# Raw weight buffers, load distance and the engine of the weight sums in the down stage of an MLP

## The chip, the cores and the metric

The kernel runs on one core of one Trainium2 chip. The metric is the device time of one execution in microseconds (us); it is the median of several runs. One further execution was recorded by the hardware profiler, and all rows come from that one.

## The reference, cut to what matters

Two layers work on 1024 + 32 = 1056 tokens of 1024 features: layer a has a state-space mixer, layer b a stick-breaking attention. Each layer ends with the same MLP, and this is all that the change touches:

```python
def sq_relu_mlp(h, w_up, w_down):
    return jnp.square(jax.nn.relu(h @ w_up)) @ w_down

for i in range(DEPTH):                       # DEPTH = 2
    ...                                      # mixer i, y += mixer(rmsnorm(y))
    y_p = y_p + sq_relu_mlp(rms_norm(y_p, norm_mlp[i]), mlp_up[i], mlp_down[i])
    y_s = y_s + sq_relu_mlp(rms_norm(y_s, norm_mlp[i]), mlp_up[i], mlp_down[i])
```

`w_up` is 1024 x 4096 and `w_down` 4096 x 1024, both float32.

## The kernel before

Activations lie transposed: features on the 128 partitions, the 1056 tokens along the free dimension, so a tile of 128 features is [128, T] with T = 1056; HW = 528 is half of the tokens, QW = 264 a quarter. `X[d]` for d = 0 to 7 is the residual stream, kept in SBUF.

Matrix products are made exact enough by splitting each float32 operand into a rounded part (`hi`, made by ScalarE) and a remainder (`lo`, made by VectorE), and by adding three products hi*hi, hi*lo, lo*hi on TensorE. One product of the MLP (`product`, L849) runs for each of its k operands three such pairs over two token quarters, so 6 matmuls of 128 x 264 per operand; with four operands these are 24 matmuls.

In the MLP a two-by-two block product is done with seven products instead of eight. This needs sums of the quarters of the weights. `wprep` (L798 to L844) makes the weights of one step in seven parts: `load` brings two raw tiles of 128 x 1024 from DRAM (`ws_...`, in buffers of the rotation `ws`, which holds two of them); `sums1` has a subtraction on GpSimd (L818, it writes half of the tile `wS`) and an addition in place on VectorE (L819); `sums2` has a subtraction on VectorE (L823) and one on GpSimd (L825, into a tile of its own, `wS4`); then four `split` parts, raw0, S, raw1 and S4, each with a rounding on ScalarE (L835) and a remainder on VectorE (L836). Where a step has fewer than four operands the tiles are narrower: 128 columns per operand and quarter.

The up stage (`project`, L971) goes through 15 pairs of output tiles; a pair has seven products of four operands. During pair p the weights of pair p+1 are made, one part after each product. The results, squared, go to DRAM as `q_d[k]` (seven halves of 528 tokens for each k = 0 to 15).

The down stage goes through 19 steps (`STEPS`). Step s adds the products of the operands in `ks` to one pair of output tiles d1, d2 of `X`. Steps 0 to 18 have 2, 3, 4, 4, 3, 3, 3, then nine times 4 (steps 7 to 15), then 3, 2 and 1 operands. In `step` (L1003) the seven products use three PSUM tiles: U, W, U, V, U, V, U. After each product VectorE adds the tile to half of an `X` tile (L1018). So the third product can't begin to write U before the addition of the first is done, the fifth not before that of the third, and the sixth not before that of the fourth. Beside product n run the n-th part of a refill and the n-th part of the weights of the next step. A refill (`refill`, L983) reads the seven halves `q_d[k]` (L993) into four tiles `y` and splits them (L718 on ScalarE, L719 on VectorE) into the operand buffers of a k that is used up. Refills r0, r1 and r2 are the operands 0, 1 and 2; r0 and r1 are made during the last pair of the up stage, r2 beside step 0, operand 3 beside step 1, and 4 to 15 beside steps 3 to 14 (step 2 and steps 15 to 18 have none). `reload` (L1063) brings the eight X tiles back from DRAM (L1066).

All DMAs are issued on SP's queue, in order. Each engine, too, takes its instructions in order. In the MLP that order isn't written out by hand: a scheduler lays the instructions out when the program is built, by their place in the source and by its own reckoning of when operands and buffers are free, so an instruction can stand in its queue well ahead of its place in the source. Waits follow from the data and from buffers being reused.

Of the kernel before, what the change touches and what calls it, by code (L numbers as in the profile page):

```python
# [7 lines left out]
F32 = mybir.dt.float32  # L8
# [4 lines left out]
ALU = mybir.AluOpType  # L13
# [5 lines left out]
T = SEQ + DEC  # L19
# [4 lines left out]
HW = T // 2  # L24
# [68 lines left out]
def hybrid_step(ctx: ExitStack, tc: tile.TileContext, xt, cst, cbf, w_in, w_dt, w_out, w_up0, w_dn0, w_qkv, w_o,  # L93
# [27 lines left out]
    rota = {"ws": [0, 1], "wh": [0, 1, 2], "wl": [0, 1, 2]}  # L121

    def wtile(kind, dt, name):

        n = rota[kind].pop(0)
        rota[kind].append(n)
        return wp.tile([128, 1024], dt, name=f"{kind}_{name}", tag=f"{kind}{n}")

    eng = [ve]
# [495 lines left out]
    def mlp_pools(st, stp, name):  # L625
        mp = st.enter_context(tc.tile_pool(name=f"mp{name}", bufs=2, reuse_waits="tile"))
        pp = stp.enter_context(tc.tile_pool(name=f"pp{name}", bufs=8, space=PSUM, reuse_waits="tile"))
        return mp, pp
# [35 lines left out]
    class Up:  # L664
# [132 lines left out]

        def wprep(self, p, loads, n=4):  # L798


            w = {}
            nm = f"{self.name}{p}"

            def view(t):
# [7 lines left out]
            def part(t, i):  # L812
                return t[:, 512 * i:512 * i + 128 * n]

            def sums1():
                r0, r1 = w["raw0"], w["raw1"]
                S = w["S"] = self.mp.tile([128, 1024], F32, name=f"wS_{nm}", tag="wS", bufs=1)
                gp.tensor_tensor(part(S, 1), part(r0, 0), part(r1, 0), op=ALU.subtract)  # L818
                ve.tensor_tensor(part(r1, 0), part(r1, 0), part(r1, 1), op=ALU.add)  # L819

            def sums2():
                r0, r1, S = w["raw0"], w["raw1"], w["S"]
                ve.tensor_tensor(part(S, 0), part(r1, 0), part(r0, 0), op=ALU.subtract)  # L823
                S4 = w["S4"] = self.mp.tile([128, 512], F32, name=f"wS4_{nm}", tag="wS4", bufs=1)
                gp.tensor_tensor(part(S4, 0), part(r0, 1), part(S, 0), op=ALU.subtract)  # L825

# [12 lines left out]
            def ready():  # L839
                (a, b, s, q) = (w[f"{x}_"] for x in ("raw0", "raw1", "S", "S4"))  # L840
                self.prepared[p] = [(a, 0), (s, 0), (a, 512), (s, 512), (b, 0), (b, 512), (q, 0)]

            return [load, sums1, sums2, lambda: split("raw0"), lambda: split("S"), lambda: split("raw1"),
                    lambda: (split("S4"), ready())]  # L844

# [124 lines left out]

        def project(self, tail):  # L971

            for p in range(1, 16):
                prep = self.up_weights(p + 1) if p < 15 else tail
                if p == 1:
                    prep.insert(3, self.mix0)
                self.pair(p, prep)

# [3 lines left out]

        def refill(self, k):  # L983

            box = {}

            def f(j):
                n = ORDER.index(j)
                if n % 2 == 0:
                    box["y"] = self.mp.tile([128, T], F32, name=f"y_{self.name}{k}{j}", bufs=2 if n < 4 else 1,  # L990
                                            tag=("sq", "sq", "acc", "u0")[n // 2])
                    for i, jj in enumerate(ORDER[n:n + 2]):
                        dma(box["y"][:, HW * i:HW * i + HW], self.q_d[k, QPOS.index(jj)])  # L993
                t = self.ttile(DTAGS[k % 4][n], f"d{j}_{self.name}{k}")
                self.split(j, ("d", k), box["y"][:, HW * (n % 2):HW * (n % 2) + HW], t[:, 0:HW], t[:, HW:T])

            return [lambda j=j: f(j) for j in ORDER]

        def down_weights(self, s):
            pair, ks = STEPS[s]  # L1000
            return self.wprep(f"d{s}", lambda i: self.w_dn[pair, i][:, :, 128 * ks[0]:128 * ks[-1] + 128], len(ks))

# [22 lines left out]
    def mlp(X, src, w_last, gain_col, w_up, w_dn, mp, pp, close_pp, stp, name, order, last=None, each=None):  # L1025

        up = Up(mp, name, gain_col, w_up, order)
        xs = [up.parts(src[i], (f"m{2 * i}", f"m{2 * i + 1}"), f"l{name}{i}") for i in range(4)]
        blk = down_block(w_last, xs, X, pp, f"l{name}", lambda d: up.add(d, X[d]))
# [29 lines left out]
        hold = [f"h{order[d]}" for d in (0, 1, 3, 5, 2, 4, 6, 7)]  # L1059
        r0, r1, r2 = (up.refill(k) for k in range(3))  # L1060
        dw = up.down_weights(0)

# [5 lines left out]
        with ExitStack() as pu:  # L1068
            up.psum = pu.enter_context(tc.tile_pool(name=f"pu{name}", bufs=4, space=PSUM, reuse_waits="tile"))
            up.project([lambda: (dw[0](), reload((0, 1))), dw[1], lambda: (run(r0[:3]), dw[2]()),  # L1070
                        lambda: (run(r0[3:6]), dw[3]()), lambda: (run(r0[6:] + r1[:3]), dw[4]()),
                        lambda: (run(r1[3:5]), dw[5](), reload((2, 3))), lambda: (dw[6](), run(r1[5:]))])
        reload(range(4, KD))
# [4 lines left out]
        with ExitStack() as pd:  # L1078
            up.psum = pd.enter_context(tc.tile_pool(name=f"pd{name}", bufs=1, space=PSUM, reuse_waits="tile"))
            up.roles = {"U": 0, "V": 2, "W": 3, "F": 1}  # L1080
            for s, (pair, _) in enumerate(STEPS):
# [593 lines left out]
```

## Time and profile before

| | us |
|---|---|
| median of 3 runs | 3089.58 (3088.73 to 3091.41) |
| profiled execution | 3097.83 |
| its span, first to last instruction | 3096.1 |
| down stage of layer a | 1310.6 to 1692.4 |
| down stage of layer b | 2727.5 to 3092.2 |

The profile names engines PE (TensorE matmuls), PEld (its weight loads), DVE (VectorE), ACT (ScalarE), POOL (GpSimd) and SP (the DMA queue). A row of the timeline has the start in us, the duration in us, the engine, the line of the kernel, the operation, the tile written, the tiles read, their sizes and how many instructions are merged in the row; in brackets, how long the engine had been idle before, and what it waited for. Times within the profile count from the first instruction. Tiles of layer a carry an a in their name, those of layer b a b; `ws_ad`, `wh_ad`, `wl_ad`, `wS_ad` are the down stage's raw weights, rounded weights, remainders and sums, `d_a` its operands, `ps_da9U` the PSUM tile U of step 9, `x_sa` the saved X.

### The profile page before, as it was taken

The numbers are of one execution on the slowest core, as the hardware profiler recorded it, in microseconds if no ns is written. First come the engines' busy times: TensorE is split into PE (matmuls) and PEld (weight loads), VectorE is DVE, ScalarE is ACT, GpSimd is POOL, SyncE is SP. The second block draws the span as 40 slices with busy tenths as digits, with TensorE's granted clock in tenths as the row PEclk, the third lists the DMA queues.
The fourth block names the chain that finished last, engine by engine and source line by source line (L and its number), as shares of the span: only waits on it lengthen the run. The fifth ranks groups of instructions, "written<-read, shape, count | busy, mean of one in ns | idle before, by whom it ended". The sixth has DMA issues, their size and how long they took to land.

```text
span 3096.1 us, 55134 instructions
## 1 busy us (share of the span) xinstructions
PE 2962.8 (96%) x22206; PEld 2809.7 (91%) x22206; DVE 2272.8 (73%) x3192; ACT 1292.1 (42%) x2207; POOL 851.6 (28%) x667
## 2 busy tenths in 40 slices
PE   9999999999999999989998999999999999989999
PEld 7899888898999999989998888888889999989999
DVE  7877778776749877767677677677678877777675
ACT  4433333434214333334333466666664433344331
POOL 2666656665100111011112023333230111111111
PEclk9999999999999999989999999999999999999999
DMA  4323333333522544554432322222234444474442
GB/s 133 71 74 77 72 79 82 81 79 93 184 90 103 176 153 143 172 182 151 136 113 93 105 78 75 66 71 71 78 119 141 150 143 139 143 240 145 128 139 84
DMA packets 191351, 360.11 MB, mean 116 GB/s; under 512 B 21772, under 2 KB 78968, under 8 KB 191096
## 3 DMA queue, kind: packets, MB, share of 16 engines
q1 hardware_dynamic: 191096, 356.59, 37.5%
q8 instruction: 175, 2.87, 0.4%
q14 instruction: 80, 0.66, 0.1%
HBM read 246.21 MB, written 101.93 MB: 112 GB/s over the span
## 4 chain that ended last, share of the span: by engine, by line
PE 64%; DVE 20%; DMA 5%; issue 5%; ACT 3%; POOL 2%; SPq 0%; DVEq 0%; POOLq 0%; ACTq 0%
PE ps_i L181 9%; PE ps_ub L857 9%; PE ps_ua L857 8%; PE ps_q L181 3%; PE ps_o L181 3%; PE ps_k L181 2%; PE o L1356 2%; PE wt L1340 2%; PE ps_v L181 2%; PE ps_o L162 2%; PE ps_lb L162 1%; PE ps_p L181 1%; DVE p L1303 1%; DMA ws_ad<-in_w_dn 1%; PE ps_la L162 1%
## 5 line engine op out<-in xcount | busy, mean ns | idle before, releaser
L181 PE MATMUL ps_i<-xh_n,wh_i 128*128 128x352 f32 x1056 | 359.9, 341 | 0.0
L181 PE MATMUL ps_i<-xl_n,wh_i 128*128 128x352 f32 x1056 | 344.4, 326 | 0.0
L181 PE MATMUL ps_i<-xh_n,wl_i 128*128 128x352 f32 x1056 | 344.3, 326 | 0.0
L1305 POOL TENSOR_TENSOR b<-b,p 128x255 f32<-128x255 f32 (+7 forms) x128 | 165.3, 1292 | 377.7 <-DVE p L1303 243.1
L1303 DVE TENSOR_TENSOR_SCAN p<-p 128x255 f32<-128x255 f32 (+7 forms) x128 | 193.2, 1510 | 90.6 <-ACT p L1301 89.5
L181 PEld LDWEIGHTS ps_i<-xh_n,wh_i 128*128 128x128 f32 x1056 | 202.4, 192 | 13.3 <-issue 11.6
L181 PEld LDWEIGHTS ps_i<-xl_n,wh_i 128*128 128x128 f32 x1056 | 203.5, 193 | 0.0
L181 PEld LDWEIGHTS ps_i<-xh_n,wl_i 128*128 128x128 f32 x1056 | 202.0, 191 | 0.0
L466 ACT ACTIVATE L<-L,naT 128x128 f32<-128x128 f32 (+1 forms) x288 | 89.7, 382 | 166.5 <-POOL L L463 166.5
L818 POOL TENSOR_TENSOR wS_a<-ws_a,ws_a 128x512 f32<-128x512 f32 x15 | 24.9, 1661 | 387.0 <-DMA ws_a<-in_w_up 372.8
L1301 ACT ACTIVATE p<-z,qn_q 128x384 f32<-128x384 f32 (+4 forms) x192 | 104.6, 579 | 60.0 <-PE z L1332 30.1
L140 POOL TENSOR_TENSOR wl_i<-ws_i,wh_i 128x1024 fp32r<-128x1024 f32 x44 | 105.4, 2395 | 73.7 <-ACT wh_i L139 73.5
L463 POOL TENSOR_TENSOR L<-ab,cs 128x512 f32<-128x512 f32 (+1 forms) x72 | 103.1, 1433 | 52.9 <-PE pb L498 43.4
L718 ACT ACTIVATE d_b<-y_b 128x528 fp32r<-128x528 f32 x112 | 70.8, 640 | 110.6 <-DMA y_b<-q_db 16.5
L718 ACT ACTIVATE d_a<-y_a 128x528 fp32r<-128x528 f32 x112 | 70.7, 640 | 107.1 <-DMA y_a<-q_da 13.8
L1340 PE MATMUL wt<-cs,b 128*128 128x128 f32 x576 | 90.4, 281 | 14.8 <-DVE wts L1345 12.3
L1301 ACT ACTIVATE b<-z,qn_q 128x384 f32<-128x384 f32 (+4 forms) x192 | 104.3, 584 | 0.0
L818 POOL TENSOR_TENSOR wS_bd<-ws_bd,ws_bd 128x512 f32<-128x512 f32 (+3 forms) x19 | 21.9, 1153 | 296.4 <-DMA ws_bd<-in_w_dn 272.1
L818 POOL TENSOR_TENSOR wS_b<-ws_b,ws_b 128x512 f32<-128x512 f32 x15 | 24.0, 1600 | 284.6 <-DMA ws_b<-in_w_up 254.6
L818 POOL TENSOR_TENSOR wS_ad<-ws_ad,ws_ad 128x512 f32<-128x512 f32 (+3 forms) x19 | 23.3, 1225 | 275.6 <-DMA ws_ad<-in_w_dn 255.8
L719 DVE TENSOR_TENSOR d_b<-y_b,d_b 128x528 fp32r<-128x528 f32 x112 | 82.0, 742 | 21.6 <-ACT d_b L718 20.9
L719 DVE TENSOR_TENSOR d_a<-y_a,d_a 128x528 fp32r<-128x528 f32 x112 | 81.0, 735 | 18.4 <-ACT d_a L718 17.5
(1650 smaller groups left out, 9734.9 us busy)
## 6 DMA issues: line engine op xcount, KB each, us to landing
y_a<-q_da SPq DMA_DIRECT2D x112, 264.0 KB
y_b<-q_db SPq DMA_DIRECT2D x112, 264.0 KB
ws_i<-in_w_in SPq DMA_DIRECT2D x48, 512.0 KB
ab<-acs_d SPq DMA_DIRECT2D x64, 256.0 KB
q_da<-t_a SPq DMA_DIRECT2D x30, 528.0 KB
q_db<-t_b SPq DMA_DIRECT2D x30, 528.0 KB
ws_a<-in_w_up SPq DMA_DIRECT2D x30, 512.0 KB
ws_b<-in_w_up SPq DMA_DIRECT2D x30, 512.0 KB
```

What stands on the lines that cost most here:

```text
L140: eng[0].tensor_tensor(lo, st, hi.bitcast(F32), op=ALU.subtract)
L162: te.matmul(box["ps"][g][:, :GW], a[:, c:c + 128], b[:, GRP[g]], start=(k == ks[0] and i == 0), stop=(k == ks[-1] and i == 2))
L181: te.matmul(box["ps"][:, :n], a[:, c:c + 128], b[:, grp[g]], start=(k == 0 and i == 0), stop=(k == nk - 1 and i == 2))
L463: gp.tensor_tensor(L[0:w, :, :w], ab[0:w, :, :w], cs[0:w, None, C_MASK:C_MASK + w].to_broadcast([w, 4, w]), op=ALU.add)
L718: sc.activation(hi, x, AF.Copy)
L719: ve.tensor_tensor(lo, x, hi.bitcast(F32), op=ALU.subtract)
L818: gp.tensor_tensor(part(S, 1), part(r0, 0), part(r1, 0), op=ALU.subtract)
L857: te.matmul(ps[:, g, :QW], a[:, c:c + 128], b[:, QW * g:QW * g + QW], start=(first and n == 0 and i == 0), stop=(n == len(ks) - 1 and i == 2),
L1301: sc.activation(t[0:np_, c:c + w], ps[0:np_, :w], AF.Sigmoid, scale=sn[0:np_, f])
L1303: ve.tensor_tensor_scan(p[0:np_, 1:W][:, ::-1], p[0:np_, 1:W][:, ::-1], p[0:np_, 1:W][:, ::-1], 1.0, op0=ALU.mult, op1=ALU.bypass)
L1305: gp.tensor_tensor(b[0:np_, 0:W - 1], b[0:np_, 0:W - 1], p[0:np_, 1:W], op=ALU.mult)
L1340: te.transpose(ps[:, c, :], self.b[:, 128 * (c0 + c):128 * (c0 + c) + 128], ident)
```

## The change

The rotation of raw weight buffers grows from two to four while an MLP runs; the two new ones live in the MLP's own pool, which loses the tile `wS4`. In the down stage the load of step s+2's weights is called at the head of step s, instead of step s+1's; the sums of step s+1's weights stay beside step s. The two subtractions that ran on GpSimd run on VectorE for the down stage's weights (`eng`), and stay on GpSimd for the up stage's. The last one (`sums3`) writes in place over half of raw0 and so comes after raw0's split. The loads of step 0's weights and r0's reads are called at the end of pair 14, step 1's weights at the head of pair 15, and the first reload of X later within pair 15. The default number of buffers of the MLP's pool is one; all other tiles in it name their own.

```diff
     def mlp_pools(st, stp, name):
-        mp = st.enter_context(tc.tile_pool(name=f"mp{name}", bufs=2, reuse_waits="tile"))
+        mp = st.enter_context(tc.tile_pool(name=f"mp{name}", bufs=1, reuse_waits="tile"))
...
-        def wprep(self, p, loads, n=4):
+        def wprep(self, p, loads, n=4, eng=None):
+            eng = eng or gp
...
             def sums1():
-                gp.tensor_tensor(part(S, 1), part(r0, 0), part(r1, 0), op=ALU.subtract)
+                eng.tensor_tensor(part(S, 1), part(r0, 0), part(r1, 0), op=ALU.subtract)
                 ve.tensor_tensor(part(r1, 0), part(r1, 0), part(r1, 1), op=ALU.add)
             def sums2():
                 ve.tensor_tensor(part(S, 0), part(r1, 0), part(r0, 0), op=ALU.subtract)
-                S4 = w["S4"] = self.mp.tile([128, 512], F32, name=f"wS4_{nm}", tag="wS4", bufs=1)
-                gp.tensor_tensor(part(S4, 0), part(r0, 1), part(S, 0), op=ALU.subtract)
+            def sums3():
+                r0, S = w["raw0"], w["S"]
+                eng.tensor_tensor(part(r0, 1), part(r0, 1), part(S, 0), op=ALU.subtract)
+                w["S4"] = r0[:, 512:]
...
-            return [load, sums1, sums2, lambda: split("raw0"), lambda: split("S"), lambda: split("raw1"),
+            return [load, sums1, sums2, lambda: split("raw0"), lambda: (sums3(), split("S")), lambda: split("raw1"),
                     lambda: (split("S4"), ready())]
...
+                if p == 14:
+                    prep += before
...
-        def refill(self, k):
+        def refill(self, k, ahead=False):
...
+            fs = [lambda n=n: f(n) for n in range(7)]
+            return [lambda: [load(n) for n in range(4)]] + fs if ahead else fs
...
         up = Up(mp, name, gain_col, w_up, order)
+        more.update({("ws", n): mp for n in (2, 3)})
+        rota["ws"] += [2, 3]
...
-            up.project([lambda: (dw[0](), reload((0, 1))), dw[1], lambda: (run(r0[:3]), dw[2]()),
-                        lambda: (run(r0[3:6]), dw[3]()), lambda: (run(r0[6:] + r1[:3]), dw[4]()),
-                        lambda: (run(r1[3:5]), dw[5](), reload((2, 3))), lambda: (dw[6](), run(r1[5:]))])
+            up.project([dws[1][0], dw[1], lambda: (run(r0[1:4]), dw[2](), reload((0, 1))),
+                        lambda: (run(r0[4:7]), dw[3]()), lambda: (run(r0[7:] + r1[:2]), dw[4]()),
+                        lambda: (run(r1[2:5]), dw[5](), reload((2, 3))), lambda: (dw[6](), run(r1[5:]))],
+                       [dw[0], r0[0]])
...
-                side = [refills.get(s, [])]
+                side = []
+                if s + 2 < len(STEPS):
+                    side.append(dws[s + 2][:1])
+                side.append(refills.get(s, []))
                 if s + 1 < len(STEPS):
-                    side.append(up.down_weights(s + 1))
+                    side.append([None] + dws[s + 1][1:])
                 up.step(s, X, side, finished)
```

## Rows read from the trace of the kernel before

**Rows 1.** The page's first part: each engine's busy time.

```profile
PE 2962.8 (96%) x22206; PEld 2809.7 (91%) x22206; DVE 2272.8 (73%) x3192; ACT 1292.1 (42%) x2207; POOL 851.6 (28%) x667
```

**Rows 2.** Stretches: length, busy us (count) PE PEld DVE ACT POOL, clock, DMA, GB/s.

```profile
985.00:1310.60 325.60, 321.13 (x2615) 319.85 (x2614) 250.26 (x337) 119.18 (x169) 44.03 (x30) 1.00 0.44 152
1310.60:1377.10 66.50, 53.17 (x381) 51.84 (x380) 44.32 (x63) 21.08 (x30) 12.38 (x6) 0.87 0.60 203
1377.10:1448.90 71.80, 68.26 (x547) 66.72 (x547) 55.82 (x80) 30.01 (x44) 9.85 (x8) 1.00 0.50 156
1448.90:1629.60 180.70, 167.13 (x1347) 165.45 (x1346) 126.75 (x160) 64.11 (x88) 23.32 (x16) 0.99 0.39 120
1629.60:1692.40 62.80, 54.46 (x422) 53.04 (x421) 45.35 (x55) 22.44 (x28) 19.00 (x11) 0.95 0.25 88
2727.50:2786.80 59.30, 50.96 (x379) 48.56 (x379) 47.53 (x67) 22.87 (x35) 8.21 (x6) 0.94 0.69 237
2786.80:2859.80 73.00, 68.31 (x548) 66.78 (x547) 55.85 (x80) 30.02 (x44) 9.57 (x8) 1.00 0.50 153
2859.80:3039.50 179.70, 167.10 (x1347) 165.42 (x1346) 126.72 (x160) 64.15 (x88) 23.34 (x16) 0.99 0.39 121
3039.50:3092.20 52.70, 52.05 (x422) 51.29 (x421) 29.33 (x47) 8.01 (x13) 5.01 (x6) 1.00 0.25 91
```

**Rows 3.** The chain of waits: start us, us, what.

```profile
1353.15 7.51 DMA ws_ad<-in_w_dn
...
1488.54 2.93 PE ps_da8V L857 x24
...
1574.88 4.61 PE ps_da12U L857 x24
```

**Rows 4.** Timeline of PE at four of its waits.

```profile
1507.69 0.76 PE L857 MATMUL ps_da9U<-d_a,wh_ad_S 128*128 128x264 f32 x4 [1.67 <-DVE X_a L1018]
...
1321.95 1.25 PE L857 MATMUL ps_da1U<-d_a,wh_ad_raw 128*128 128x264 f32 x4 [3.88 <-ACT wh_ad_raw L835]
...
1365.83 1.25 PE L857 MATMUL ps_da2U<-d_a,wh_ad_S 128*128 128x264 f32 x4 [6.22 <-DVE X_a L1018]
...
2736.02 0.50 PE L857 MATMUL ps_db0V<-d_b,wh_bd_raw 128*128 128x264 f32 x2 [4.08 <-ACT d_b L718]
```

**Rows 5.** Timeline of DVE in step 10 of layer a.

```profile
1517.66 1.23 DVE L836 TENSOR_TENSOR wl_ad_raw<-ws_ad,wh_ad_raw 128x1024 fp32r<-128x1024 f32 x1 [0.19 <-ACT wh_ad_raw L835]
...
1524.74 0.69 DVE L819 TENSOR_TENSOR ws_ad<-ws_ad 128x512 f32<-128x512 f32 x1 [2.93 <-POOL wS_ad L818]
1525.35 0.70 DVE L1018 TENSOR_TENSOR X_a<-X_a,ps_da10W 128x528 f32<-128x528 f32 x1
...
1527.18 2.31 DVE L836 TENSOR_TENSOR wl_ad_raw<-ws_ad,wh_ad_raw 128x1024 fp32r<-128x1024 f32 x1
1529.42 0.69 DVE L1018 TENSOR_TENSOR X_a<-X_a,ps_da10U 128x528 f32<-128x528 f32 x1
```

**Rows 6.** Timeline of POOL in the same step.

```profile
1523.41 1.29 POOL L818 TENSOR_TENSOR wS_ad<-ws_ad,ws_ad 128x512 f32<-128x512 f32 x1 [17.47 <-DMA ws_ad<-in_w_dn]
1526.79 1.62 POOL L825 TENSOR_TENSOR wS_ad<-ws_ad,wS_ad 128x512 f32<-128x512 f32 x1 [2.09 <-DVE wS_ad L823]
```

**Rows 7.** Timeline of SP's queue in the same step: issues.

```profile
1518.91 0.55 SPq L810 DMA_DIRECT2D ws_ad<-in_w_dn  x1
```

**Rows 8.** DMA queues from 1300 to 1345: packets, MB, share of 16 engines.

```profile
q1 hardware_dynamic: 6352, 13.70, 88.1%
```

**Rows 9.** Timeline of SP's queue in the up stage and in step 0.

```profile
1012.47 0.32 SPq L993 DMA_DIRECT2D y_a<-q_da  x1
...
1024.86 2.26 SPq L993 DMA_DIRECT2D y_a<-q_da  x4
...
1314.09 1.21 SPq L810 DMA_DIRECT2D ws_ad<-in_w_dn  x2
...
1318.76 6.87 SPq L1066 DMA_DIRECT2D X_a<-x_sa  x4
1325.69 5.18 SPq L993 DMA_DIRECT2D y_a<-q_da  x7
```

More of the change, by code (lines that the diff above doesn't have):

```diff
@@ L121, in hybrid_step @@
     rota = {"ws": [0, 1], "wh": [0, 1, 2], "wl": [0, 1, 2]}
+    more = {}
     def wtile(kind, dt, name):
@@ L126, in wtile @@
         rota[kind].append(n)
-        return wp.tile([128, 1024], dt, name=f"{kind}_{name}", tag=f"{kind}{n}")
+        return more.get((kind, n), wp).tile([128, 1024], dt, name=f"{kind}_{name}", tag=f"{kind}{n}")
     eng = [ve]
@@ L969, in parts, with project @@
             return hi, lo
-        def project(self, tail):
+        def project(self, tail, before):
             for p in range(1, 16):
@@ L976, in project, with load, f @@
                     prep.insert(3, self.mix0)
+                if p == 14:
+                    prep += before
                 self.pair(p, prep)
-        def refill(self, k):
[L985 to L993, printed above, removed]
+        def refill(self, k, ahead=False):
+            ys = []
+            def load(n):
+                y = self.mp.tile([128, T], F32, name=f"y_{self.name}{k}_{n}", bufs=2 if n < 2 else 1,
+                                 tag=("sq", "sq", "acc", "u0")[n])
+                for i, j in enumerate(ORDER[2 * n:2 * n + 2]):
+                    dma(y[:, HW * i:HW * i + HW], self.q_d[k, QPOS.index(j)])
+                ys.append(y)
+            def f(n):
+                j = ORDER[n]
+                if n % 2 == 0 and len(ys) == n // 2:
+                    load(n // 2)
                 t = self.ttile(DTAGS[k % 4][n], f"d{j}_{self.name}{k}")
-                self.split(j, ("d", k), box["y"][:, HW * (n % 2):HW * (n % 2) + HW], t[:, 0:HW], t[:, HW:T])
-            return [lambda j=j: f(j) for j in ORDER]
+                self.split(j, ("d", k), ys[n // 2][:, HW * (n % 2):HW * (n % 2) + HW], t[:, 0:HW], t[:, HW:T])
+            fs = [lambda n=n: f(n) for n in range(7)]
+            return [lambda: [load(n) for n in range(4)]] + fs if ahead else fs
         def down_weights(self, s):
             pair, ks = STEPS[s]
-            return self.wprep(f"d{s}", lambda i: self.w_dn[pair, i][:, :, 128 * ks[0]:128 * ks[-1] + 128], len(ks))
+            return self.wprep(f"d{s}", lambda i: self.w_dn[pair, i][:, :, 128 * ks[0]:128 * ks[-1] + 128],
+                              len(ks), ve)
         def step(self, s, X, side, each):
@@ L1059, in mlp @@
         hold = [f"h{order[d]}" for d in (0, 1, 3, 5, 2, 4, 6, 7)]
-        r0, r1, r2 = (up.refill(k) for k in range(3))
-        dw = up.down_weights(0)
+        r0, r1, r2 = up.refill(0, True), up.refill(1), up.refill(2)
+        dws = [up.down_weights(s) for s in range(len(STEPS))]
+        dw = dws[0]
         def reload(ds):
@@ L1091, in finished @@
                         done(d)
-                side = [refills.get(s, [])]
+                side = []
+                if s + 2 < len(STEPS):
+                    side.append(dws[s + 2][:1])
+                side.append(refills.get(s, []))
                 if s + 1 < len(STEPS):
-                    side.append(up.down_weights(s + 1))
+                    side.append([None] + dws[s + 1][1:])
                 up.step(s, X, side, finished)
+        for n in (2, 3):
+            rota["ws"].remove(n)
         return stp.enter_context(tc.tile_pool(name=f"pk{name}", bufs=8, space=PSUM, reuse_waits="tile"))
```

## The prediction, made before the change was run

> **What bounds the kernel now.** I read the page first: TensorE is busy 96% of the span [rows 1], so what can be won must lie in stretches where it is not, and the change edits two of them, the down stages of layers a and b. The view by stretches [rows 2] shows how much lies there. A product of four operands is 24 matmuls and takes 2.93 us when nothing is in its way [rows 3]: 0.122 us a matmul. The stretches hold 378, 546, 1344 and 420 matmuls (7 products x 6 x the operands of the steps), so they need 46.0, 66.4, 163.5 and 51.1 us. They take 66.5, 71.8, 180.7 and 62.8 us in layer a and 59.3, 73.0, 179.7 and 52.7 in layer b. Lost: 20.5 + 5.4 + 17.2 + 11.7 = 54.8 us in a, 13.3 + 6.6 + 16.2 + 1.6 = 37.7 us in b, 92.5 us together. The up stage loses hardly anything: 321 us busy of 326 [rows 2].
>
> Then TensorE's own waits [rows 4]. In steps 7 to 14 there is one of size in each step, always at the same place, before the fifth product, for VectorE's addition of the third into X; sixteen of them, 1.3 to 2.1 us, 26.2 us in all. In the first steps they have other names: ScalarE's rounding of the weights (3.88), an addition into X (6.22), the operands (4.08).
>
> VectorE's timeline says why the addition is late [rows 5]. It stands idle 2.93 us before L819, because L819 needs the GpSimd difference of L818; two operations start 0.61 us apart, so the queue behind it (a sum, a refill, a 1024-wide rounding remainder) then runs late, and that remainder takes 2.31 us where another of the same shape takes 1.23: the second GpSimd subtraction runs beside it [rows 6]. GpSimd had itself waited 17.47 us for a weight load [rows 6]. That load was issued at 1518.91 [rows 7], the moment its buffer's last reader ended (1517.66 + 1.23 [rows 5]), and landed some 4.4 us later. So the chain is: two raw buffers, a load that can't start before the previous step's weights are split, GpSimd, VectorE in order, the addition, TensorE.
>
> **The change part by part.**
>
> *Four buffers, loads two steps ahead.* The load for step s+2 is issued at the head of step s, into buffers that held step s's weights. These are read for the last time when their last pieces are split, around the end of step s-1 (1518.89 for one that was wanted at 1523 [rows 5, 6]). The load then has about 18 us before its sums are due, and takes 4 to 7.5 [rows 6, 7, 3]. So the load leaves the path in steps 2 to 18. On SP's queue it now stands ahead of the refills' reads; should it block there until 1519 in the step shown, they serve a step that starts 20 us later, so I price this at nothing.
>
> *Sums on VectorE.* Two subtractions a step leave GpSimd. On VectorE each costs its issue distance, 0.61 us at 512 wide [rows 5], and by width (an estimate) 0.46, 0.31 and 0.2 in the smaller steps: 11 x 1.22 + 5 x 0.92 + 2 x 0.62 + 0.4 = 19.7 us a layer, 39 us in all, on the engine whose lateness is the wait. Against it the 2.93 us of idle time and the 1.08 us by which the remainder was stretched go. In steps 7 to 14 VectorE works 126.75 / 8 = 15.8 us a step [rows 2]; it becomes 15.8 + 1.4 - 1.1 = 16.1 of 20.4, and an addition has 2.9 us until TensorE misses it. In steps 3 to 6 it becomes about 56 of 66.4. Nothing saturates, so I take the added work as covered by VectorE's idle time; without that cover it costs its 39 us.
>
> The Trainium skill, page "Perfetto Trace Analysis", section "Optimizing Scalar/DVE Operations", advises the other direction: work may be moved from VectorE to ScalarE or even GpSimd when VectorE is saturated, though the two share a read port. By that rule's condition the sums would come out slower by up to the 39 us above; the trace shows the condition unmet (70% busy in steps 7 to 14 [rows 2]).
>
> *What remains in steps 7 to 14.* The lost 33.4 us are the 26.2 of waits, two places where a wait was followed by matmuls at the lower clock level, 1.2 GHz (a product of 4.61 us instead of 2.93 [rows 3], 3.4 for both), and 3.8 us of smaller pieces. The nearest row for a VectorE this busy without such waits is the up stage: 250 of 326 us busy (77%), TensorE 98.6% [rows 2]. That is 0.3 us a step, 5 in sixteen. Gain 28 us; bounds 14 (half of the waits find another late instruction) and 33.
>
> *Steps 0 to 2.* Here weights come late through a crowded DMA: the transfer engines are 88% busy between 1300 and 1345 [rows 8]. Layer a's step 1 weights are issued at 1314.09 [rows 9] and TensorE waits 3.88 us for them; step 3's raw weights take 7.51 us [rows 3] and TensorE waits 6.22 through the same VectorE queue [rows 4]. Both loads now come a step or more earlier. What is late next are step 1's operands, r2: five of its seven reads are issued from 1325.69, behind four reloads of X [rows 9], and nothing of that is moved. Landing takes about as long as the weight load in the same crowd (7.51 us [rows 3]), so step 1's third product can't start much before 1332.5 and the step ends near 1343.5 (five products of 2.2 us) instead of 1347. Step 2 then needs 21 instead of 30 us. Gain in a 3.5 + 9 = 12, bounds 0 and 18. In b the operands are the first wait already (4.08 us [rows 4]); the earlier weights free only their own place in the queue, some 2 us, and 2.5 us of smaller waits: 4.5, bounds 0 and 10.
>
> *First operands during the up stage.* The source asks for r0's seven reads in the last pair, but they are issued at 1012 to 1027, at the start of the up stage [rows 9]: the order of a queue isn't the order of the source. Moving them in the source to the pair before changes nothing: 0. If the change delayed them to where the source now has them, they would still be a pair early.
>
> *Steps 3 to 6.* 12.0 us are lost, part through the same GpSimd chain; VectorE gets to 85% there, above the 77% of the up stage, so I take less than half, 5 us (bounds 0 and 10).
>
> *Steps 15 to 18.* Layer a loses 11.7 us, b only 1.6. In a GpSimd works 19.0 us for the next norm against 5.0 in b [rows 2], and that stays. Only the sums go: 2.5 us (0 to 6).
>
> *Up stage.* More buffers let loads start earlier, where nothing waits; the last GpSimd subtraction comes after the first split instead of before it, but still within the same pair of 168 matmuls (20.4 us), and its result is split only at that pair's end. Price 0, bounds 3 us either way.
>
> Sum: 28 + 12 + 4.5 + 5 + 2.5 = 52 us. Against the profiled execution, 3097.8 us (span 3096.1 and 1.7 around it), that gives 3045.8. The median of the runs lies 8.2 us lower, and I take the same difference off: **3038 us**.
>
> **The rivals.**
>
> *Half of it (gain 10 to 35, 3066 at the middle).* The late addition finds another in-order neighbour: with sums, refills and splits on VectorE its order is new, and half of each wait stays (14 us gained in steps 7 to 14); at the start the operands are late and steps 0 to 2 gain 5, the rest 4. For: four reads and reloads on one crowded queue [rows 8, 9]. Against: 4 us of slack a step.
>
> *Nearly all of it (gain above 68, about 3015).* Waits vanish, the lower clock with them (0.87 over steps 0 to 2 of a [rows 2]), and the start no longer holds: 33 + 28 + 10 + 3 = 74. Against: r2's place behind X.
>
> *VectorE becomes the bound, slower.* Each moved sum stands ahead of an addition into X that TensorE waits for, and the waits only change their name. Place: the fifth product of a step. Price: up to 39 us, less some contention: 3089.6 + 30 = about 3120. It decides once a step's VectorE work exceeds 20.4 us (15.3 in steps 4 to 6). For: it is an in-order queue that already makes the late addition. Against: 16.1 of 20.4.
>
> *No change (3085 to 3095).* The loads aren't ahead in fact, as r0's place shows that source order isn't queue order: if the new loads are queued behind waiting reads on SP, GpSimd's wait becomes VectorE's own wait for the same DMA. Against: the buffers are free 18 us before the need.
>
> **How the numbers follow.** Forecast (gain 35 to 68) 0.62; half 0.17; nearly all 0.10; no change 0.06; slower 0.05. A measurement of this kernel can tell about 0.2% (6 us) from no change. Faster 0.62 + 0.17 + 0.10 = 0.89, same 0.06, slower 0.05. The low bounds of the terms add to 14 + 0 + 0 + 0 + 0, the high ones to 77; neither end will come together, so the range is a gain of 20 to 72: 3018 to 3070. It leaves out no change, slower, and the outer parts of the two neighbours.
>
> **What would show it.** In the profile after: no L818 or L825 subtraction on GpSimd in the down stages, no VectorE wait for one; the wait before the fifth product gone from steps 7 to 14, so that a step takes 20.5 to 21 us instead of 22.5; the two long waits of layer a's start gone, with a wait for r2's operands in step 1 in their place. I am wrong on the steady part if a wait for X of a microsecond or more remains in each step, and on the start if step 2 of layer a still ends 60 us or more after step 0 began.

## The result and the profile after

The changed kernel takes 3040.6 us (median of 4 runs, 3034.7 to 3048.1) against 3089.5 for the kernel before: a ratio of 0.984, with a 95% interval of 0.982 to 0.987. The forecast was 3038. Between the two profiled executions, 3097.8 and 3043.1 us, the gain is 54.8 us; the forecast's sum was 52.

First the page's line of busy times, answering to [rows 1], and then the down stages by stretches (columns as in [rows 2]; each stretch runs from the first matmul of step 0, 3, 7 or 15 to the next; layer a first). The change shifts the line numbers: in the changed kernel and in the kernels made from it, L813 is the load L810 of before, L821, L822, L826 and L830 are the sums L818, L819, L823 and L825, L841 and L842 the split L835 and L836, L720 and L721 the split L718 and L719, L863 the matmul L857, L999 the read L993 and L1032 the addition L1018.

```profile
PE 2951.4 (97%) x22206; PEld 2805.2 (92%) x22206; DVE 2272.5 (75%) x3268; ACT 1288.2 (42%) x2207; POOL 768.8 (25%) x591
...
1313.40:1369.10 55.70, 49.15 (x379) 47.69 (x379) 47.64 (x72) 20.34 (x31) 0.00 (x0) 0.97 0.71 242
1369.10:1437.50 68.40, 67.24 (x548) 66.55 (x547) 57.36 (x87) 30.00 (x44) 0.00 (x0) 1.00 0.54 165
1437.50:1600.90 163.40, 163.40 (x1346) 163.40 (x1345) 127.12 (x178) 64.01 (x88) 0.00 (x0) 1.00 0.42 132
1600.90:1663.50 62.60, 54.37 (x421) 52.84 (x420) 46.11 (x58) 22.49 (x27) 12.78 (x5) 0.95 0.24 82
2699.90:2754.80 54.90, 49.08 (x380) 47.83 (x379) 48.50 (x74) 22.12 (x34) 0.00 (x0) 0.97 0.73 246
2754.80:2821.60 66.80, 66.68 (x549) 66.49 (x548) 57.36 (x87) 30.14 (x45) 0.00 (x0) 1.00 0.55 170
2821.60:2985.00 163.40, 163.40 (x1347) 163.40 (x1346) 127.11 (x178) 64.03 (x89) 0.00 (x0) 1.00 0.42 132
2985.00:3037.20 52.20, 51.57 (x422) 51.14 (x420) 30.89 (x51) 8.01 (x13) 0.00 (x0) 1.00 0.23 84
```

GpSimd has no work left in the down stages except the next norm's in a. TensorE is busy in the whole of steps 7 to 14: they take what 1344 matmuls need. Before, the same eight rows read 66.5, 71.8, 180.7, 62.8 and 59.3, 73.0, 179.7, 52.7 [rows 2]. The gain by stretch, a and b together (from first matmul to first matmul, and to the last one's end):

| steps | gain us | forecast |
|---|---|---|
| 0 to 2 | 10.8 + 4.4 = 15.2 | 16.5 |
| 3 to 6 | 3.4 + 6.2 = 9.6 | 5 |
| 7 to 14 | 17.3 + 16.3 = 33.6 | 28 |
| 15 to 18 | 0.1 + 0.3 = 0.4 | 2.5 |
| outside the down stages | -3.8 | 0 |

The sum, 54.9 before rounding, is the difference of the spans (3096.1 and 3041.2). The -3.8 may be scatter: layer a's down stage begins 2.7 us later than before, at 1313.4, and in the other profiles of kernels with the same or nearly the same up stage it begins anywhere from 1310.6 to 1315.5.

What the steady steps look like now, in VectorE's and TensorE's timelines of step 9 in layer a (columns as in [rows 4, 5]):

```profile
1485.30 1.23 DVE L842 TENSOR_TENSOR wl_ad_raw<-ws_ad,wh_ad_raw 128x1024 fp32r<-128x1024 f32 x1 [0.20 <-ACT wh_ad_raw L841]
1486.44 0.70 DVE L721 TENSOR_TENSOR d_a<-y_a,d_a 128x528 fp32r<-128x528 f32 x1
1487.06 0.69 DVE L830 TENSOR_TENSOR ws_ad<-ws_ad,wS_ad 128x512 f32<-128x512 f32 x1
1487.66 0.70 DVE L1032 TENSOR_TENSOR X_a<-X_a,ps_da9U 128x528 f32<-128x528 f32 x1
...
1490.04 0.65 PE L863 MATMUL ps_da9U<-d_a,wh_ad_S 128*128 128x264 f32 x4
```

The third product's addition ends at 1488.36, and the fifth product (1490.04) comes after it with 1.68 us to spare. Before (step 10), the addition ended at 1530.11 [rows 5], and the fifth product began at 1530.16 after a wait of 1.76:

```profile
1530.16 0.51 PE L857 MATMUL ps_da10U<-d_a,wh_ad_S 128*128 128x264 f32 x2 [1.76 <-DVE X_a L1018]
```

The remainder takes 1.23 again, not 2.31.

### The profile page after: what moved, and what is told of

It is laid out like the page before. It is cut to its first block, busy times and chain, and to the rows that moved or that the text cites. A ratio compares the mean times of both kernels' runs of the same rounds, so it can differ in the third digit from the quotient of the medians.

```text
span 3041.2 us, 54987 instructions
## 1 busy us (share of the span) xinstructions
PE 2951.4 (97%) x22206; PEld 2805.2 (92%) x22206; DVE 2272.5 (75%) x3268; ACT 1288.2 (42%) x2207; POOL 768.8 (25%) x591
## 4 chain that ended last, share of the span: by engine, by line
PE 78%; DVE 11%; issue 5%; DMA 3%; ACT 2%; POOL 1%; SPq 0%; DVEq 0%; ACTq 0%; POOLq 0%
PE ps_i L183 13%; PE ps_ua L863 9%; PE ps_ub L863 9%; PE ps_q L183 3%; PE ps_o L183 3%; PE ps_k L183 2%; PE o L1379 2%; PE wt L1363 2%; PE ps_o L164 2%; PE ps_v L183 1%; PE ps_p L183 1%; PE ps_lb L164 1%; PE ps_la L164 1%; DVE p L1326 1%; PE pb L500 1%
## 5 line engine op out<-in xcount | busy, mean ns | idle before, releaser
L142 POOL TENSOR_TENSOR wl_i<-ws_i,wh_i 128x1024 fp32r<-128x1024 f32 x44 | 106.5, 2421 | 71.9 <-ACT wh_i L141 71.8
L465 POOL TENSOR_TENSOR L<-ab,cs 128x512 f32<-128x512 f32 (+1 forms) x72 | 103.4, 1437 | 54.9 <-PE pb L500 45.7
L720 ACT ACTIVATE d_b<-y_b 128x528 fp32r<-128x528 f32 x112 | 70.5, 639 | 94.1 <-DMA y_b<-q_db 19.9
L720 ACT ACTIVATE d_a<-y_a 128x528 fp32r<-128x528 f32 x112 | 70.3, 639 | 92.3 <-DMA y_a<-q_da 18.8
L267 POOL TENSOR_TENSOR acc_n<-acc_n,sq_n 128x1056 f32<-128x1056 f32 x6 | 15.8, 2628 | 368.6 <-ACT sq_n L263 368.5
L1363 PE MATMUL wt<-cs,b 128*128 128x128 f32 x576 | 90.3, 280 | 15.4 <-DVE wts L1368 12.8
L1363 PEld LDWEIGHTS wt<-cs,b 128*128 128x128 f32 x576 | 64.9, 140 | 31.3 <-DVE wts L1368 13.9
L721 DVE TENSOR_TENSOR d_b<-y_b,d_b 128x528 fp32r<-128x528 f32 x112 | 77.7, 704 | 21.3 <-ACT d_b L720 21.3
L721 DVE TENSOR_TENSOR d_a<-y_a,d_a 128x528 fp32r<-128x528 f32 x112 | 77.5, 703 | 21.1 <-ACT d_a L720 21.0
L821 POOL TENSOR_TENSOR wS_a<-ws_a,ws_a 128x512 f32<-128x512 f32 x15 | 33.5, 2236 | 228.7 <-DVE xl_ua L203 145.9
L1366 ACT ACTIVATE wts<-wt 128x512 f32<-128x512 f32 (+3 forms) x128 | 66.6, 520 | 25.2 <-PE wt L1363 23.6
```

The costliest lines, as they stand in the source:

```text
L142: eng[0].tensor_tensor(lo, st, hi.bitcast(F32), op=ALU.subtract)
L465: gp.tensor_tensor(L[0:w, :, :w], ab[0:w, :, :w], cs[0:w, None, C_MASK:C_MASK + w].to_broadcast([w, 4, w]), op=ALU.add)
L720: sc.activation(hi, x, AF.Copy)
L721: ve.tensor_tensor(lo, x, hi.bitcast(F32), op=ALU.subtract)
L1363: te.transpose(ps[:, c, :], self.b[:, 128 * (c0 + c):128 * (c0 + c) + 128], ident)
```

## Experiments: what the steady steps needed

The question was which part of the chain in the prediction (the late load, GpSimd's two subtractions, the stretched remainder) makes the wait. Four kernels undo one part of the change, or do one part alone. Beside the first two the kernel before takes 3102.1 us (3096.0 to 3105.8) and the changed kernel 3042.9 (3037.0 to 3044.8).

**Four buffers and early loads, sums still on GpSimd.**

```diff
-                              len(ks), ve)
+                              len(ks), gp)
```

> The changed kernel with one part undone: the down stage's two weight subtractions go back to GpSimd (last argument of the weight preparation in down_weights). Four raw buffers and loads two steps ahead stay. Theory (the late load is the root, GpSimd and VectorE's order only pass it on): the waits before the fifth product of steps 7 to 14 shrink from 1.3-2.1 us to under 0.5, because the subtractions no longer wait for a DMA, and what is lost is only the stretched remainders (1.1 us of VectorE a step): time 3042 to 3052. Rival (the engine is the root: GpSimd's 1.3 to 1.6 us subtractions and their contention with VectorE make the addition late even with the weights in place): steps of 21.5 us or more, time 3060 to 3080.

Measured: 3053.1 us (3051.2 to 3058.3), 0.985 of before (0.9835 to 0.9866). Steps 7 to 14 take 163.4 us in both layers, no more than in the changed kernel. Step 9, in GpSimd's, VectorE's and TensorE's timelines:

```profile
1474.41 1.64 POOL L821 TENSOR_TENSOR wS_ad<-ws_ad,ws_ad 128x512 f32<-128x512 f32 x1 [7.14 <-DVE wl_ad_S L842]
1485.95 1.69 POOL L830 TENSOR_TENSOR ws_ad<-ws_ad,wS_ad 128x512 f32<-128x512 f32 x1 [9.90 <-DVE wl_ad_raw L842]
...
1476.08 0.69 DVE L822 TENSOR_TENSOR ws_ad<-ws_ad 128x512 f32<-128x512 f32 x1 [1.19 <-POOL wS_ad L821]
1486.71 0.70 DVE L1032 TENSOR_TENSOR X_a<-X_a,ps_da9U 128x528 f32<-128x528 f32 x1 [0.22 <-PE ps_da9U L863]
...
1489.44 0.65 PE L863 MATMUL ps_da9U<-d_a,wh_ad_S 128*128 128x264 f32 x4
```

VectorE still waits for GpSimd, 1.2 us in almost every step, but ten microseconds ahead of the addition that counts. That one even waits for TensorE, and leaves 2.03 us to spare. So a wait on VectorE for GpSimd isn't in itself what cost the time. The rival's steps of 21.5 us or more did not come; the time is 1 us above the theory's range.

**Two buffers and late loads, both sums on VectorE.**

```diff
-        def wprep(self, p, loads, n=4):
+        def wprep(self, p, loads, n=4, eng=gp):
...
-                gp.tensor_tensor(part(S, 1), part(r0, 0), part(r1, 0), op=ALU.subtract)
+                eng.tensor_tensor(part(S, 1), part(r0, 0), part(r1, 0), op=ALU.subtract)
...
-                gp.tensor_tensor(part(S4, 0), part(r0, 1), part(S, 0), op=ALU.subtract)
+                eng.tensor_tensor(part(S4, 0), part(r0, 1), part(S, 0), op=ALU.subtract)
...
-            return self.wprep(f"d{s}", lambda i: self.w_dn[pair, i][:, :, 128 * ks[0]:128 * ks[-1] + 128], len(ks))
+            return self.wprep(f"d{s}", lambda i: self.w_dn[pair, i][:, :, 128 * ks[0]:128 * ks[-1] + 128], len(ks), ve)
```

> The kernel before with one part of the change alone: the down stage's two weight subtractions on VectorE; two raw buffers, loads one step ahead, and the first operands as before. Theory (the late load is the root): VectorE now waits for the DMA itself, at the same place, so a wait of 1 us or more stays before the fifth product of steps 7 to 14; about 1.1 us of contention goes: 3065 to 3085. Rival (the engine is the root): most of the gain is here already, 3040 to 3055.

Measured: 3048.2 us (3042.9 to 3051.2), 0.983 (0.9813 to 0.9847). Steps 7 to 14: 163.4 us again. Step 9, VectorE and TensorE:

```profile
1485.06 0.69 DVE L818 TENSOR_TENSOR wS_ad<-ws_ad,ws_ad 128x512 f32<-128x512 f32 x1 [1.43 <-DMA ws_ad<-in_w_dn]
1488.64 0.70 DVE L1018 TENSOR_TENSOR X_a<-X_a,ps_da9U 128x528 f32<-128x528 f32 x1
1489.26 0.68 DVE L823 TENSOR_TENSOR wS_ad<-ws_ad,ws_ad 128x512 f32<-128x512 f32 x1
...
1490.08 0.65 PE L857 MATMUL ps_da9U<-d_a,wh_ad_S 128*128 128x264 f32 x4
```

The load is as late as before and VectorE stands still for it, 1.43 us here and 1.0 to 1.7 in the sixteen steps; the addition ends 0.74 us early all the same (0.45 to 1.16). Here the rival's time came true, and in the run before it the theory's steps: neither the late load nor the engine is the root alone. The scheduler also laid VectorE's queue out anew: L823, which ran ahead of the addition before (at 1525.96), stands behind it now.

**One of the two subtractions alone.** The kernel before, with only L818 moved to VectorE, and with only L825 moved; one run each.

> The kernel before (two raw buffers, loads one step ahead) with only the first of the two weight subtractions of the down stage on VectorE; the last one stays on GpSimd. Theory (a threshold: an addition into X may come 2.9 us late before TensorE misses it, so cutting either half of the chain load - GpSimd - VectorE ends the wait whole): VectorE itself waits for the load, but the addition of the third product starts about 1527.0 in the time of the step that was shown, before 1528.3, and the stretch of steps 7 to 14 takes 163 to 166 us instead of 180.7. Rival (the parts add: two subtractions, half of the gain each): 170 to 174 us.

> The kernel before with only the last weight subtraction of the down stage on VectorE; the first stays on GpSimd, so GpSimd still waits for the load and VectorE for GpSimd. Theory (threshold): nothing stretches the remainder any more and it no longer stands ahead of the addition, which starts about 1527.8 and ends some 0.1 us after TensorE asks for it: a wait of 0.1 to 0.5 us a step, steps 7 to 14 in 164 to 168 us. Rival (the parts add): 170 to 174 us. Second rival (the wait for GpSimd's first subtraction alone is the whole cause): 178 to 181.

Measured: 3049.4 and 3066.9 us, with the kernel before at 3099.8 beside them. Steps 7 to 14: 163.4 us with L818 moved, 165.3 in either layer with L825 moved. Both are the threshold's forecasts, and not those of parts that add (170 to 174). VectorE's addition and TensorE's fifth product in step 9, first with L818 moved, then with L825 moved:

```profile
1489.41 0.70 DVE L1018 TENSOR_TENSOR X_a<-X_a,ps_da9U 128x528 f32<-128x528 f32 x1
1490.76 0.65 PE L857 MATMUL ps_da9U<-d_a,wh_ad_S 128*128 128x264 f32 x4
```

```profile
1494.16 0.69 DVE L819 TENSOR_TENSOR ws_ad<-ws_ad 128x512 f32<-128x512 f32 x1 [2.95 <-POOL wS_ad L818]
1497.21 0.70 DVE L1018 TENSOR_TENSOR X_a<-X_a,ps_da9U 128x528 f32<-128x528 f32 x1
1497.82 1.22 DVE L836 TENSOR_TENSOR wl_ad_raw<-ws_ad,wh_ad_raw 128x1024 fp32r<-128x1024 f32 x1
1497.96 0.76 PE L857 MATMUL ps_da9U<-d_a,wh_ad_S 128*128 128x264 f32 x4
```

With L825 moved VectorE keeps its whole wait for GpSimd, 2.95 us (2.93 in [rows 5]), yet seven eighths of the loss are gone: the remainder is not stretched (1.22) and stands behind the addition now, where it stood ahead of it in [rows 5]. The addition ends at 1497.91; the fifth product was due 5.85 us after the third began (1491.80), at 1497.65, so 0.26 us is what is left of the wait. Step 9 is the worst of the eight: over all of them the fifth product begins 1.2 us late, and it takes about 0.1 us longer in each; together that is about the 1.9 us by which 165.3 exceeds 163.4. Most of this gain is the new order: from L819 to the addition it was 4.68 us in [rows 5] and is 3.05 here, because the remainder's 2.24 went out of this stretch and L825's 0.60 came in. An estimate from these rows: a remainder that was no longer stretched, but had kept its place at 1.14 us, would have won only 0.5.

Set in a row, the end of the addition against the moment at which TensorE is ready for the fifth product (step 9 of layer a, but for the first line; over all sixteen steps it is -1.3 to -2.1 before, and in the kernels with 163.4 never under +0.40):

| kernel | spare us | steps 7 to 14 of a, us |
|---|---|---|
| before (step 10) | -1.7 | 180.7 |
| only L825 on VectorE | -0.26 | 165.3 |
| only L818 on VectorE | +0.65 | 163.4 |
| two buffers, both on VectorE | +0.74 | 163.4 |
| changed kernel | +1.68 | 163.4 |
| four buffers, both on GpSimd | +2.03 | 163.4 |

That is a threshold, not a sum: an addition may end up to 2.9 us after its product (the fourth product's length) and costs nothing, and only what goes beyond that is paid. Before, it was 1.7 us beyond. Each of these edits takes about that much or more out of the chain and pays in full, or nearly so; the second one pays nothing there. How much of each is the edit itself and how much the scheduler's new order is not shown, as no run held the order fixed.

## Experiments: the start of the down stage

Here the halves do differ. Steps 0 to 6 (the border inside them is blurred where a product of step 3 is queued early), in us for a and b; the matmuls need 112.4:

| kernel | a | b |
|---|---|---|
| before | 138.3 | 132.3 |
| only L825 on VectorE | 132.3 | 131.7 |
| only L818 on VectorE | 128.2 | 128.6 |
| two buffers, both on VectorE | 125.6 | 126.4 |
| four buffers, both on GpSimd | 125.3 | 128.0 |
| changed kernel | 124.1 | 121.7 |
| changed kernel, once more | 124.0 | 122.0 |

Each half (four buffers with early loads, or both sums on VectorE) gains 17 to 19 us over both layers and the two together 24.8: they overlap, but both are wanted. Here, and not in the steady steps, each half alone falls behind the changed kernel: by 7.5 and 6.1 us, of 8 between the spans of the profiles. By the medians of the runs beside it each half is 10 and 5 us slower; the 5 us of two buffers are not clear of scatter (3042.9 to 3051.2 against 3037.0 to 3044.8).

Three kernels took apart what had been moved in the source. The changed kernel was run again beside the first of them, with the kernel before at 3102.1 us; beside the other two, and beside those on the tail of layer a, the kernel before takes 3100.1 (3090.5 to 3112.9).

> The changed kernel itself, beside the three others on the same chip: 3035 to 3048, as measured before. It serves as their reference, and shows how far its own runs scatter.

Measured: 3042.9 us (3037.0 to 3044.8), 0.981 (0.9795 to 0.9828); every stretch within 0.5 us of the first profile.

**Loads called one step ahead, in four buffers.**

```diff
...
-                if s + 2 < len(STEPS):
-                    side.append(dws[s + 2][:1])
...
-                    side.append([None] + dws[s + 1][1:])
+                    side.append(dws[s + 1])
```

> The changed kernel with the loads of the down stage's weights called one step ahead again instead of two (step 0's at the head of the last pair, step 1's in step 0); four buffers and the sums on VectorE stay. Theory (the buffers free the load; where the source calls it matters little, since an instruction is queued as early as its buffers allow): within 6 us of the changed kernel in the same job, steps 7 to 14 at 20.4 us. Rival (the two-step distance is needed): waits for the load reappear, 3055 to 3075.

Measured: 3042.0 us (3038.7 to 3048.6), 0.981 (0.9791 to 0.9834); steps 0 to 6 take 121.3 and 123.0. No difference: with the buffers there, the loads come early without being called early. The first of step 1's two loads, in the changed kernel and then in this one:

```profile
1292.36 0.56 SPq L813 DMA_DIRECT2D ws_ad<-in_w_dn  x1
```

```profile
1293.39 0.56 SPq L813 DMA_DIRECT2D ws_ad<-in_w_dn  x1
```

**r0's reads called in the last pair again.**

> The changed kernel with the third part undone: r0's reads are called where they were before, in the last pair of the up stage. Theory (the reads are queued at the start of the up stage either way): no difference from the changed kernel beyond 0.2%, r0's seven reads issued between 1010 and 1035. Rival (calling them a pair earlier is what relieves the start of the down stage): steps 0 to 2 of either layer 3 us or more longer than the 55.7 and 54.9 us of the changed kernel, time 3046 to 3055 where the changed kernel takes 3043.

Measured: 3040.6 us (3037.2 to 3047.7), 0.981 (0.9773 to 0.9846). SP's timeline, the changed kernel first, then this one:

```profile
1015.66 0.32 SPq L999 DMA_DIRECT2D y_a<-q_da  x1
```

```profile
1016.56 0.32 SPq L999 DMA_DIRECT2D y_a<-q_da  x1
```

They are issued some 280 us before the place at which the source calls them (the last pair begins about 1293), in both, as in [rows 9].

**The reload of X 4 to 7 called at the ends of steps 0 and 1**, so that r2's reads don't stand behind it.

```diff
-        reload(range(4, KD))
...
+                if s < 2:
+                    side.append([None] * 6 + [lambda: reload((4 + 2 * s, 5 + 2 * s))])
```

> The changed kernel with one thing moved: the reloads of X 4 to 7, called before step 0, are called at the end of steps 0 (X 4, 5) and 1 (X 6, 7), just ahead of the steps that add into them. Theory (r2's reads stand behind these four reloads on SP's queue, and step 1 waits for them): steps 0 to 2 shorten by 3 to 7 us in each layer (46.0 is needed, 55.7 and 54.9 are taken): time 3029 to 3040 where the changed kernel takes 3043. Rival (the transfers themselves are the limit, whatever their order, or ScalarE's and VectorE's own work in steps 0 and 1): within 2 us a layer.

Measured: 3046.3 us (3042.5 to 3050.3), 0.983 (0.9791 to 0.986); steps 0 to 2 take 57.7 and 55.3, no less than 55.7 and 54.9. Six of r2's reads did move up, from 1328.79 to 1319.56, and the wait for r2's operands in step 1 was gone. The time wasn't.

**Less to transfer.**

```diff
-                dma(X[d], up.x_s[d])
+                if d < 2:
+                    dma(X[d], up.x_s[d])
+                else:
+                    dma(X[d][:, :QW], up.x_s[d][:, :QW])
+                    gp.memset(X[d][:, QW:], 0.0)
```

> Leaves out three quarters of the reload of X 2 to 7 (each reload brings 264 of 1056 columns, GpSimd sets the rest to zero), 2.4 MB less in each layer around the start of the down stage; so those rows of X are not the reference's. The changed kernel takes 55.7 us (layer a) and 54.9 (b) for steps 0 to 2, where the matmuls need 46.0. If the amount that the transfer engines have to move there is the limit (they are 88% busy), steps 0 to 2 become 3 to 6 us shorter in each layer and the refill's reads land within about 3 us of their issue. If instead the engines' in-order chains of reads, roundings and sums are the limit, steps 0 to 2 change by less than 1.5 us. Steps 7 to 14 stay at 163.4 us in both.

Measured (one run): 3044.1 us, with the kernel before at 3103.6 beside it. Its two stretches of steps 0 to 2, the DMA queue from 1303 to 1348 (the changed kernel's, then its own), and TensorE's first waits:

```profile
1310.60:1364.50 53.90, 49.12 (x381) 47.62 (x380) 47.23 (x73) 21.01 (x33) 3.04 (x4) 0.97 0.63 200
2699.90:2756.30 56.40, 50.26 (x381) 48.65 (x380) 48.13 (x74) 22.60 (x35) 2.98 (x4) 0.94 0.62 202
...
q1 hardware_dynamic: 6186, 13.61, 88.5%
q1 hardware_dynamic: 6606, 11.95, 82.3%
...
1317.56 0.64 PE L863 MATMUL ps_da1U<-d_a,wh_ad_raw 128*128 128x264 f32 x3 [2.40 <-ACT wh_ad_raw L841]
1319.42 1.25 PE L863 MATMUL ps_da0U<-d_a,wh_ad_S 128*128 128x264 f32 x4 [1.23 <-DVE X_a L1032]
```

Layer a takes 1.8 us less, more than the 1.5 that was allowed for, and b 1.5 more; together 110.3 us against 110.6. So by this one run the amount on the queue isn't the limit. GpSimd's zeros did not disturb VectorE: L721 took its usual 0.70 us at 1320.51, though a filling ran from 1320.04 to 1320.80. The same two waits stand in the changed kernel (TensorE, then ScalarE, VectorE):

```profile
1320.47 0.75 PE L863 MATMUL ps_da1U<-d_a,wh_ad_raw 128*128 128x264 f32 x4 [2.59 <-ACT wh_ad_raw L841]
1322.23 1.25 PE L863 MATMUL ps_da0U<-d_a,wh_ad_S 128*128 128x264 f32 x4 [1.00 <-DVE X_a L1032]
1335.02 0.51 PE L863 MATMUL ps_da1U<-d_a,wh_ad_raw 128*128 128x264 f32 x2 [1.09 <-ACT d_a L720]
...
1319.04 0.64 ACT L720 ACTIVATE d_a<-y_a 128x528 fp32r<-128x528 f32 x1 [0.96 <-DMA y_a<-q_da]
1319.59 0.83 ACT L841 ACTIVATE wh_ad_raw<-ws_ad 128x768 fp32r<-128x768 f32 x1
...
1318.38 0.70 DVE L788 TENSOR_TENSOR t_a<-f_a 128x528 f32<-128x528 f32 x1
...
1321.48 0.70 DVE L1032 TENSOR_TENSOR X_a<-X_a,ps_da0U 128x528 f32<-128x528 f32 x1
```

Step 1's weights are there (their load is issued at 1292.36 and 1294.56 now, not at 1314.09 as in [rows 9]), but ScalarE's rounding stands behind the last piece of r1, whose read has just landed. And step 0's first addition, whose product was through at about 1315, stands on VectorE behind what closes the up stage (L788 and its neighbours, no gap from 1314.5 to 1323.9). What is left at the start thus looks like the two engines' order of work at the border of the stages. That is read off the rows; no run here changed that order, so it isn't shown. In layer b, too, TensorE's first wait is now one for an addition, and the wait for the operands, 4.08 us in [rows 4], is down to 0.84:

```profile
2705.68 0.72 PE L863 MATMUL ps_db0U<-d_b,wh_bd_S 128*128 128x264 f32 x4 [2.53 <-DVE X_b L1032]
...
2707.48 0.56 PE L863 MATMUL ps_db0U<-d_b,wh_bd_S 128*128 128x264 f32 x2 [0.84 <-ACT d_b L720]
```

## Experiments: the tail of layer a

In steps 15 to 18 of layer a GpSimd's additions for the next norm (L267) run beside VectorE (GpSimd, then VectorE, in the changed kernel; L206 is a split of X for that norm):

```profile
1637.89 2.56 POOL L267 TENSOR_TENSOR acc_n<-acc_n,sq_n 128x1056 f32<-128x1056 f32 x1 [10.46 <-ACT sq_n L263]
1652.18 5.21 POOL L267 TENSOR_TENSOR acc_n<-acc_n,sq_n 128x1056 f32<-128x1056 f32 x2 [8.66 <-ACT sq_n L263]
...
1638.66 2.35 DVE L842 TENSOR_TENSOR wl_ad_raw<-ws_ad,wh_ad_raw 128x512 fp32r<-128x512 f32 x1
1641.55 3.09 DVE L206 SCALAR_TENSOR_TENSOR xl_n<-X_a,cs,xh_n 128x1056 fp32r<-128x1056 f32 x1
1652.45 2.65 DVE L842 TENSOR_TENSOR wl_ad_raw<-ws_ad,wh_ad_raw 128x256 fp32r<-128x256 f32 x1
```

**These additions on VectorE**, and once with the later reload too.

```diff
-                (ve if self.n == KD - 1 else gp).tensor_tensor(self.acc, self.acc, s, op=ALU.add)
+                ve.tensor_tensor(self.acc, self.acc, s, op=ALU.add)
```

> The changed kernel with the next norm's six additions of squares (128 x 1056, 2.6 us each on GpSimd) put on VectorE; four of them run in steps 16 to 18 of layer a. Theory (the stall of steps 15 to 18 in layer a, 62.6 us for 51, is VectorE stretched by GpSimd: remainders of 2.4 and 2.7 us for 0.7 and 0.4, splits of 3.1 and 2.9 for 1.3): these 62.6 us become 56 to 60, time 3037 to 3041 where the changed kernel takes 3043. Rival (the splits of X for the norm are the load, wherever the sums run): no gain, or a loss, as VectorE gets 1.3 us more for each.

> Both edits together, the reloads of X 4 to 7 later and the norm's additions on VectorE. They act in different stretches (steps 0 to 2 of both layers, steps 15 to 18 of layer a), so their gains should add: 3024 to 3036 by the theories above, 3043 by the rivals.

Measured: 3043.9 us (3036.4 to 3045.3), 0.981 (0.9777 to 0.9848), and 3041.4 (3037.6 to 3043.6), 0.981 (0.9768 to 0.985). The stretch of steps 15 to 18 with the additions on VectorE:

```profile
1597.80:1657.60 59.80, 53.85 (x422) 52.82 (x420) 44.48 (x64) 22.62 (x28) 0.00 (x0) 0.97 0.24 86
```

59.8 us instead of 62.6, with six more operations on VectorE and less time busy (44.48 against 46.11). Such 2.8 us lie within what the runs differ by, so neither kernel counts as faster; no version tried here beats the changed kernel by more than that. The stretch itself did get shorter: from the first matmul to the last one's end it takes 60.0 and 60.4 us in these two profiles, and 62.9 to 63.3 in the six of the changed kernel and its other variants with both sums on VectorE. That is the lower edge of the theory's gain (62.6 to become 56 to 60).

## Why the prediction was right, and where it was not

**The whole.** 48.9 us by the medians and 54.8 by the profiles, against 52. The 8.2 us taken off for the profiled execution were too many: the profile after lies 2.4 above its median. The kernel before also differs more from one set of runs to another (3089 and 3102) than the changed one (3041 and 3043). That the sum came out so near is in part luck: its terms are off by +5.6 (steps 7 to 14), +4.6 (3 to 6), -1.3 (0 to 2), -2.1 (15 to 18) and -3.8 (outside), and these cancel.

**Steps 7 to 14: right mechanism, term mis-sized, 28 for 33.6.** The rest of 0.3 us a step, taken from the up stage, doesn't exist here: the wait, the lower clock and the pieces all went. A busy VectorE (127.1 / 8 = 15.9 us a step; 16.1 was worked out) costs TensorE nothing while no addition is over 2.9 us late, so the up stage's share of idle time was the wrong row. The chain was named rightly, but as if load, GpSimd and stretching each had a share; the runs show that one edit of it, with the order that came with it, was enough. The second half of the change is not needed for these 33.6 us.

**VectorE as cover, right.** In steps 7 to 14 sums of 8 x 1.22 = 9.8 us a layer, at the prediction's price, went onto VectorE for nothing. The Trainium skill, page "Perfetto Trace Analysis", section "Optimizing Scalar/DVE Operations", ties the move the other way to a saturated VectorE. The trace agrees: at 78% busy (127.1 of 163.4) it shows no cost of having it all there.

**Steps 0 to 2, right in size (15.2 for 16.5), half right in reason.** In layer a the 3.5 us up to the end of step 1 did not come: it ends 36.1 us after step 0 began, and did so after 36.4 before. The gain came in step 2, some 10 us (9 forecast). There the wait for step 3's weights went, as said (6.22 before, none there now). A crowded DMA was only part of that wait: the load was issued at 1352.51, when L825 ended, and L825 had taken 5.14 us instead of 1.62 (the last section has the rows). Step 1's wait for its weights did not go: 3.88 became 2.59, where by the rows above the rounding stands behind r1's last piece. A wait for r2's operands in step 1 came as foretold, but of 1.09 us; with r2's reads ahead of X it went and gained nothing, so "r2's place behind X" is refuted as what limits. In b the size is right (4.4 for 4.5) and the reason isn't: the operands' wait mostly went, and waits for additions (2.53 and 1.64 us) took its place. No run took b's start apart.

**Steps 3 to 6, 9.6 for 5.** The fear of an 85% busy VectorE (84 to 86% came) was largely baseless: of the 66.4 us needed, b lost 0.4 on top and a 2.0.

**Steps 15 to 18, 0.4 for 2.5: wrong.** The sums weren't what these steps wait for; the norm's additions are part of it, and they stayed. The prediction also misread [rows 2]: of GpSimd's 19.0 us in a only 12.8 were the norm's, as the row after shows, and the 5.0 in b were sums.

**r0's reads, 0: right**, shown by the run that moves them back. Loads two steps ahead in the source: nothing by itself; the prediction gave that to the buffers and the place together, and it belongs to the buffers.

## What to carry to other kernels

Where an engine feeds another through a buffer with slack, measure the lateness at the one hand-over that counts, against the moment the consumer is ready: only what exceeds the slack is paid, and the cheapest edit that gets under it wins all of it. Two edits that break the same chain are not worth the sum of their gains, so time each alone. In a kernel whose queues are laid out by a scheduler, an edit can win by the new order that comes with it, as the moved remainder did here; read the place of an instruction from the trace: giving it buffers moved the loads, moving the call in the source did not.

## What the hardware showed beside that

A VectorE operation that reads two SBUF tiles and began while GpSimd ran an addition was stretched, far beyond the 1.08 us of [rows 5]: 128x256 took 2.65 us (0.42 with the additions on VectorE), 128x512 took 2.35 (0.69), and the 1056 wide one 3.09 (1.31). It ended within 1.2 us of GpSimd's. The addition into X, which reads one SBUF tile and PSUM, was not stretched: 0.70 us at 1486.71 with GpSimd's L830 running from 1485.95 to 1487.64. The Trainium skill, page "SBUF — State Buffer", section "Who interferes with whom", says this of VectorE instructions with two SBUF inputs and clears those with one. The rows agree with both halves.

Which of the two is held depends, in these rows, on which was running first. A VectorE operation that was running when GpSimd began was not stretched: L721, 0.70 us from 1485.79, ahead of L830 above. And GpSimd itself can be held. In layer a before the change its subtraction, begun while VectorE's L719 ran (from 1347.12), took 5.14 us, while VectorE ran one such operation after the other at their usual lengths; it ended 1.23 us after the next addition into X had begun (GpSimd, then VectorE):

```profile
1347.34 5.14 POOL L825 TENSOR_TENSOR wS_ad<-ws_ad,wS_ad 128x512 f32<-128x512 f32 x1 [6.13 <-DVE wS_ad L823]
...
1348.36 1.21 DVE L836 TENSOR_TENSOR wl_ad_raw<-ws_ad,wh_ad_raw 128x1024 fp32r<-128x1024 f32 x1
1351.25 0.69 DVE L1018 TENSOR_TENSOR X_a<-X_a,ps_da1U 128x528 f32<-128x528 f32 x1
```
